# Gathering the value products of a retention pair, and zeros ahead of the first projection, in a two-layer hybrid encoder

## The chip, the core and the metric

The kernel runs on one core of one Trainium2 chip. The metric is the device time of one execution in microseconds (us), lower is better. Before the change it is 1287.65 us, the median of three runs (1287.47 to 1289.41).

## What is computed

Two encoder layers act on x with 512 positions and 1024 channels. Each layer first projects RMSNorm(x) with one matrix into retention queries, keys, values and gates (eight heads of 64 channels) and into queries, keys and values of four differential-attention heads. The retention is written in chunks; within a chunk every head needs masked scores times values, and a state from the other chunks is added:

```python
scores = jnp.einsum('bnthd,bnshd->bnhts', qc, kc) * dmask[None, None]
intra = jnp.einsum('bnhts,bnshd->bnthd', scores, vc)
...
out = (intra + cross_f + cross_b).reshape(B, S, H, D)
```

Both groups are normed per head, joined and projected back (`w_out`), then a SwiGLU block with 2816 inner channels follows. All is float32.

## The kernel before, in words

Activations lie transposed, channels on the partitions, so x is eight tiles of 128x512. For most products a float32 operand is split in two, hi (a rounded copy of type fp32r, made by ACT in `split_chunk` L166, `split_scaled` L185 or `split` L192) and lo (the rest, made by DVE in L167, L186, L193). `mm3` (L173 to L176) then issues three fp32r products for each, hi*hi, hi*lo and lo*hi. Weights come in chunks of 128x1024 through three `raw` buffers, all issued from SP's queue (L152).

A layer has five stages. `project_first` makes four projections from the eight tiles of x, interleaved, while these still arrive: for each tile 12 products of 512 columns, 96 in all. In layer 0 the loads for it are issued at L661 to L668, alternating half a weight chunk (L152) and a tile of x (L115), after the load of the parameters `prm_sb` (L109); all are on SP. The rows of the norm follow (L223), then attention heads woven with the other projections (L586). Then comes the **retention stage**: L617 weaves the generator `pairs` with fillers, which are the remaining projections (`acc` banks) and the first half of the output projection (L604, also `acc` banks). The second half of the output projection (L623) needs the results `mix[0]` to `mix[3]` of the four pairs, and the feed-forward block (L629 on) needs the output projection.

`ret_pair` (L404) handles two heads and yields after each of its steps. Step 1 (to L436) makes the decay weights, the state `r` from a float32 product (L430), and the split queries and keys. Step 2 (L439 to L460) makes for each head a mask `arg` (L442 to L444), and then, for each half c of the 512 positions, eight score products (L454) into two `sc` banks, one a head, and two maskings on DVE (L457), one a head, into a tile `sm`. Tiles `sm` come from the ring `ah` of three buffers. Step 3 (L462 to L476) opens the bank `o` with two float32 products of the state (L463, L464) and adds the eight value products (L469): for each half c and each chunk j one for head 0, which writes partitions 0 to 63 of the bank, and one for head 1, which writes partitions 64 to 127. They are plain float32, 64 columns of weights, 256 columns moved. The trace records each float32 product as two matmuls, so a pair's eight value products are 16 records, and the two layers' eight pairs have 128. Step 4 (L478 on) squares, sums over partitions (L128, L129), norms, gates (L481, L482) and splits the result into `mix`.

`PAIRS` (L36) interleaves these steps over the pairs. What order an engine's queue has in the end is not set by the order of the code alone: the program is built by a planner with a simulated clock (L756), which issues on each engine, in order of the code, what is ready at that moment of the simulation. A dependency made with `order` (L94) asks for an order in the plan alone; it puts no wait on the chip. The data dependencies carry the waits.

PSUM has four tags of two banks: `acc`, `sc`, `o` and `aux`.

Of the kernel before, what the change touches and what calls it, by code (L numbers as in the profile page):

```python
# [9 lines left out]
F32R = mybir.dt.float32r  # L10
# [3 lines left out]
P = 128  # L14
# [22 lines left out]


NW, NQK, NMIX, NAH, NHL = 12, 11, 20, 3, 3


PRM_AG, PRM_FG, PRM_RG, PRM_QG, PRM_KG, PRM_DG = 0, 16, 32, 34, 36, 38
# [9 lines left out]
def encoder_kernel(ctx: ExitStack, tc: tile.TileContext, xT, wfirst, wsingle, wvv, wout, wgu, wdn, prm, lam, cst, outT):  # L52
    nc = tc.nc
# [10 lines left out]
    def nm(s):  # L64
        uid[0] += 1
        return f"{s}{uid[0]}"

    def big(s, dt=F32, tag="w", bufs=NW):
        return tpool.tile([P, T], dt, tag=tag, name=nm(s), bufs=bufs)
# [4 lines left out]
    def bank(tag, bufs):  # L74
        return psum.tile([P, 512], F32, tag=tag, name=nm(tag), bufs=bufs)
# [4 lines left out]
    aux_bank = lambda: bank("aux", 2)  # L80
# [8 lines left out]
    def f32(ap):  # L89
        return ap.bitcast(F32)  # L90
# [3 lines left out]
    order = mybir.DependencyInfo(mybir.DependencyClass.NoSync, mybir.DependencyReason.DATA)  # L94
# [11 lines left out]


    prm_sb = cpool.tile([P, PRM_N], F32, name="prm_sb")
    nc.sync.dma_start(prm_sb, prm)  # L109
    cst_sb = cpool.tile([P, CST_N], F32, name="cst_sb")  # L110
    xscr = ctx.enter_context(tc.tile_pool(name="dpool", bufs=1, space=bass.MemoryType.DRAM)).tile([KT, P, T], F32, name="xscr")

    def load_x(src, kt):
        xt = big("x", tag="qk", bufs=NQK)
        nc.sync.dma_start(xt, src[kt])  # L115
        return xt

    ndist = cst_sb[:, CST_DIST : CST_DIST + 896]
# [38 lines left out]
            load_piece(new, src, i)  # L157
        return new

    def split_chunk(raw, n, pieces):  # L160
        hi = wpool.tile([P, 1024], F32R, tag="hi", name=nm("hi"), bufs=NHL)
        lo = wpool.tile([P, 1024], F32R, tag="lo", name=nm("lo"), bufs=NHL)
        q = n // pieces
        for i in range(pieces):
            s = slice(i * q, (i + 1) * q)
            nc.scalar.copy(hi[:, s], raw[:, s])  # L166
            nc.vector.tensor_tensor(lo[:, s], raw[:, s], f32(hi[:, s]), op=ALU.subtract)  # L167
        return hi, lo

    def chunk(*a, **kw):  # L170
        return split_chunk(*load_chunk(*a, **kw))

    def mm3(out, L, R, start, stop):  # L173
        nc.tensor.matmul(out, L[0], R[0], start=start, stop=False)  # L174
        nc.tensor.matmul(out, L[0], R[1], start=False, stop=False)  # L175
        nc.tensor.matmul(out, L[1], R[0], start=False, stop=stop)  # L176

    def cut(pair, *idx):
        return tuple(t[idx] for t in pair)
# [99 lines left out]
    def layer(l, n1, h, x_src, first_raw):  # L279


        def project_first():
            banks = [b() for b in (acc_bank, acc_bank, sc_bank, sc_bank)]
            for c in range(4):
                w = [t.rearrange("p (k f) -> p k f", f=512) for t in split_chunk(*first_raw[c])]
                for k in range(2):
                    kt = 2 * c + k
                    for i, ps in enumerate(banks):
                        mm3(ps, cut(w, slice(None), k, slice(i * P, (i + 1) * P)), h[kt], kt == 0, kt == KT - 1)
            return banks  # L290
# [8 lines left out]
        first = project_first()  # L299
# [104 lines left out]
        def ret_pair(pr):  # L404
            qT, kT, v = rqs[pr], rks[pr], rv
            lgc = lambda d, hh: lg[:, l * 16 + d * 8 + 2 * pr + hh : l * 16 + d * 8 + 2 * pr + hh + 1]
            lgp = lambda d: lg[:, 32 + l * 8 + d * 4 + pr : 32 + l * 8 + d * 4 + pr + 1]

            wq = big("wq")
            func(wq[:, :C], qpos[:, :C], AF.Exp, scale=lgp(1))  # L410
            func(wq[:, C:], qpos[:, C:], AF.Exp, scale=lgp(0))
            qw = wq
            nc.vector.tensor_tensor(qw, qT, wq, op=ALU.mult)

            tp = aux_bank()
            for j in range(4):
                nc.tensor.transpose(tp[:, j * P : (j + 1) * P], kT[:, j * P : (j + 1) * P], ident)
            kw = big("kw")
            nc.vector.tensor_tensor(
                kw.rearrange("p (j h d) -> p j h d", j=4, h=2),  # L420
                tp.rearrange("p (j h d) -> p j h d", j=4, h=2),
                wk[:, l, :, 2 * pr : 2 * pr + 2].rearrange("p j (h o) -> p j h o", o=1).broadcast_to([P, 4, 2, HD]),
                op=ALU.mult,
            )
            kv = aux_bank()
            e = slice((pr % 2) * P, (pr % 2 + 1) * P)
            for d in range(2):
                for j in range(2):
                    jj = 2 * d + j
                    nc.tensor.matmul(kv[:, d * P : (d + 1) * P], kw[:, jj * P : (jj + 1) * P], v[pr // 2][jj][:, e], start=j == 0, stop=j == 1)  # L430
            r = rs[pr % 2]
            kvv = kv[:, : 2 * P].rearrange("p (d e) -> p d e", d=2)
            for hh in range(2):
                b = slice(hh * HD, (hh + 1) * HD)
                nc.vector.tensor_copy(r[b, :, b], kvv[b, :, b])
            qs, ks = stack_one(qT, "mix", NMIX), stack_two(kT, "mix", NMIX)  # L436
            yield

            both = []  # L439
            for hh in range(2):  # L440
                arg = big("arg")
                nc.vector.tensor_scalar(arg[:, :384], dneg, lgc(1, hh), None, op0=ALU.mult)  # L442
                nc.vector.scalar_tensor_tensor(arg[:, :384], dpos, lgc(0, hh), arg[:, :384], op0=ALU.mult, op1=ALU.add)
                func(arg[:, :384], arg[:, :384], AF.Exp)  # L444
                both.append(bass.AP(arg.tensor, arg.offset, [arg.ap[0], [P, 2], [1, C]]))
            s = []
            for c in range(2):
                ps = [sc_bank() for _ in range(2)]
                for j in range(2):
                    for hh in range(2):  # L450
                        out = ps[hh][:, (1 - j) * C : (2 - j) * C]
                        sb, tb = slice((2 * c + j) * P, (2 * c + j + 1) * P), slice(c * C, (c + 1) * C)
                        for part in range(2):
                            nc.tensor.matmul(out, ks[hh][part][:, sb], qs[hh][:, tb], start=part == 0, stop=part == 1)  # L454
                sm = tpool.tile([P, 2, T], F32, tag="ah", name=nm("sm"), bufs=NAH)
                for hh in range(2):
                    nc.vector.tensor_tensor(  # L457
                        sm[:, hh].rearrange("p (j t) -> p j t", j=2), ps[hh].rearrange("p (j t) -> p j t", j=2), both[hh], op=ALU.mult
                    )
                s.append(sm)  # L460
            yield
            o = out_bank()  # L462
            nc.tensor.matmul(o[:, :C], r[:, 1, :], qw[:, :C], start=True, stop=False, skip_group_check=True)  # L463
            nc.tensor.matmul(o[:, C:], r[:, 0, :], qw[:, C:], start=False, stop=False, skip_group_check=True)  # L464
            for c in range(2):
                for j in range(2):
                    for hh in range(2):
                        b = slice(hh * HD, (hh + 1) * HD)
                        nc.tensor.matmul(  # L469
                            o[b, c * C : (c + 1) * C],  # L470
                            v[pr // 2][2 * c + j][:, (pr % 2) * P + hh * HD : (pr % 2) * P + (hh + 1) * HD],
                            s[c][:, hh, (1 - j) * C : (2 - j) * C],
                            start=False,
                            stop=(c == 1 and j == 1),
                            skip_group_check=True,
                        )  # L476
            yield
            ss = aux_bank()  # L478
            sq = square_sums(ss, consts["bones_r"], o)
            rsqrt(sq, ss, 1.0 / HD)  # L480
            nc.vector.scalar_tensor_tensor(sq, o, prm_sb[:, PRM_RG + l : PRM_RG + l + 1], sq, op0=ALU.mult, op1=ALU.mult)  # L481
            nc.vector.tensor_tensor(sq, sq, gates[pr], op=ALU.mult)  # L482
            mix[pr] = split(sq, "mix", NMIX)
            yield "norm"
# [60 lines left out]
        q, k = [None] * 4, [None] * 4  # L545
# [83 lines left out]
        for a0, a1 in FFN:  # L629
            act = []  # L630
            for ff in range(a0, a1):
                pgu = []
                for gu in range(2):
                    w = [t.rearrange("p (k f) -> p k f", f=P) for t in chunk(wgu[l, ff, gu])]
# [12 lines left out]
            for m in range(KT):  # L647
                w = chunk(wdn[l, m][:, a0 * P : a1 * P], (a1 - a0) * P)
# [12 lines left out]
    n, h, raws = Norm(), [], []  # L661
    for kt in range(KT):
        if kt % 2 == 0:
            raws.append(new_chunk(1024, 2))
        load_piece(raws[-1], wfirst[0, kt // 2], kt % 2)
        xt = load_x(xT, kt)
        h.append(split_scaled(xt, prm_sb[:, PRM_AG + kt : PRM_AG + kt + 1], "h", 16))
        n.add(xt)  # L668
    for l in range(DEPTH):
        if l:  # L670
            raws = [load_chunk(wfirst[l, c]) for c in range(4)]
        n, h = layer(l, n, h, xT if l == 0 else xscr, raws)
# [87 lines left out]
```

## Time and profile before

| | us |
|---|---|
| median of 3 runs | 1287.65 |
| the profiled execution | 1287.41 |
| its span, first to last instruction | 1285.6 |
| PE busy in it | 1271.1 |
| DVE busy | 769.2 |
| ACT busy | 570.5 |

The span is the time between the first and the last instruction; the execution's own time has 1.8 us around it. PE is the matmul engine, PEld its weight load, DVE the vector engine, ACT the scalar engine, POOL the general engine, SP the queue that issues transfers. Matmuls are pipelined: a record of 0.39 us can be followed by the next 0.23 us later, so prices below are taken from start to start.

### The profile page before, as it was taken

To read this page: it belongs to the slowest core of one execution; us is meant where nothing else is said; L and a number is where in the kernel's file an instruction comes from. 1 tells how busy PE (TensorE), PEld (TensorE's weight loads), DVE (VectorE), ACT (ScalarE), POOL (GpSimd) and SP (SyncE) were. 2 spreads that over 40 slices of the span, in tenths; PEclk is the share of its full clock that TensorE was granted. 3 is DMA by queue.
4 is the path that set the end of the run, shared out by engine and by line. 5 is a ranking of instruction groups with operands and counts; after the bars stand their busy time and mean duration, and the time that the engine had idled before them with its cause. 6 is when DMAs were issued, how large, how long until landed. Compare 5 with 4: busy or idle time off the path is not lost.

```text
span 1285.6 us, 15670 instructions
## 1 busy us (share of the span) xinstructions
PE 1271.1 (99%) x6192; PEld 1055.3 (82%) x6192; DVE 769.2 (60%) x1191; ACT 570.5 (44%) x887; POOL 17.3 (1%) x38
## 2 busy tenths in 40 slices
PE   8999999999999999999999999999999999999998
PEld 6888998678888888888888889977788888888887
DVE  6899759857443444344648997687664434443443
ACT  6777646544321222123438785564543223221221
POOL 1000000000000000000000000000000000000000
PEclk9999999999999999999999999999999999999999
DMA  7222224112333332332432122141233333333322
GB/s 263 82 67 66 67 66 148 36 64 98 99 94 103 99 98 82 114 91 85 160 109 83 50 83 66 56 141 50 66 101 96 98 98 98 98 98 98 93 80 90
DMA packets 36793, 120.07 MB, mean 93 GB/s; under 512 B 4208, under 2 KB 4208, under 8 KB 36592
## 3 DMA queue, kind: packets, MB, share of 16 engines
q1 hardware_dynamic: 36720, 119.08, 29.5%
q8 instruction: 48, 0.79, 0.3%
q14 instruction: 25, 0.20, 0.0%
HBM read 114.87 MB, written 4.19 MB: 93 GB/s over the span
## 4 chain that ended last, share of the span: by engine, by line
PE 97%; DVE 1%; ACT 1%; issue 0%; DMA 0%; SPq 0%
PE acc L174 15%; PE acc L175 14%; PE acc L176 14%; PE o L174 8%; PE o L176 8%; PE o L175 8%; PE sc L174 7%; PE sc L176 7%; PE sc L175 7%; PE sc L369 2%; PE o L469 2%; PE sc L454 1%; PE aux L385 1%; PE aux L128 1%; PE aux L129 1%; PE aux L430 1%
## 5 line engine op out<-in xcount | busy, mean ns | idle before, releaser
L166 ACT CAST hi<-raw 128x1024 fp32r<-128x1024 f32 (+2 forms) x212 | 215.7, 1019 | 510.0 <-issue 154.9
L174 PE MATMUL acc<-hi,hi 128*128 128x512 f32 (+1 forms) x914 | 337.3, 370 | 5.9 <-ACT hi L185 5.6
L175 PE MATMUL acc<-lo,hi 128*128 128x512 f32 (+1 forms) x914 | 338.3, 370 | 0.0
L176 PE MATMUL acc<-hi,lo 128*128 128x512 f32 (+1 forms) x914 | 337.7, 370 | 0.0
L167 DVE TENSOR_TENSOR lo<-raw,hi 128x1024 fp32r<-128x1024 f32 (+2 forms) x212 | 250.3, 1182 | 45.3 <-ACT hi L166 44.9
L174 PEld LDWEIGHTS acc<-hi,hi 128*128 128x128 f32 x914 | 172.6, 189 | 36.3 <-ACT hi L185 5.6
L175 PEld LDWEIGHTS acc<-lo,hi 128*128 128x128 f32 x914 | 172.5, 189 | 29.6 <-issue 1.2
L176 PEld LDWEIGHTS acc<-hi,lo 128*128 128x128 f32 x914 | 172.6, 189 | 29.2 <-issue 1.2
L174 PE MATMUL o<-hi,hi 128*128 128x512 f32 (+1 forms) x438 | 163.8, 374 | 2.2 <-DVE sq L481 2.2
L175 PE MATMUL o<-lo,hi 128*128 128x512 f32 (+1 forms) x438 | 163.6, 374 | 0.0
L176 PE MATMUL o<-hi,lo 128*128 128x512 f32 (+1 forms) x438 | 163.6, 374 | 0.0
L174 PE MATMUL sc<-hi,hi 128*128 128x512 f32 x408 | 159.4, 392 | 0.3 <-ACT hi L166 0.3
L176 PE MATMUL sc<-hi,lo 128*128 128x512 f32 x408 | 159.3, 390 | 0.0
L175 PE MATMUL sc<-lo,hi 128*128 128x512 f32 x408 | 159.2, 390 | 0.0
L174 PEld LDWEIGHTS o<-hi,hi 128*128 128x128 f32 x438 | 82.3, 188 | 17.6 <-DVE sq L481 2.7
L175 PEld LDWEIGHTS o<-lo,hi 128*128 128x128 f32 x438 | 82.4, 188 | 14.7
L176 PEld LDWEIGHTS o<-hi,lo 128*128 128x128 f32 x438 | 82.3, 188 | 14.6
L174 PEld LDWEIGHTS sc<-hi,hi 128*128 128x128 f32 x408 | 76.9, 189 | 18.6 <-issue 1.5
L176 PEld LDWEIGHTS sc<-hi,lo 128*128 128x128 f32 x408 | 76.9, 188 | 16.1
L175 PEld LDWEIGHTS sc<-lo,hi 128*128 128x128 f32 x408 | 76.9, 188 | 15.9
L103 ACT ACTIVATE sc<-sc,mx 128x512 f32<-128x512 f32 x64 | 46.0, 720 | 16.8 <-DVE mx L373 16.4
L599 DVE TENSOR_TENSOR x<-x,acc 128x512 f32<-128x512 f32 x36 | 24.6, 685 | 39.4 <-PE acc L176 39.3
(133 smaller groups left out, 1289.1 us busy)
## 6 DMA issues: line engine op xcount, KB each, us to landing
raw<-in_wgu SPq DMA_DIRECT2D x88, 512.0 KB, 3.5
raw<-in_wsingle SPq DMA_DIRECT2D x32, 512.0 KB, 3.5
raw<-in_wdn SPq DMA_DIRECT2D x32, 512.0 KB, 3.5
raw<-in_wvv SPq DMA_DIRECT2D x16, 512.0 KB, 3.5
raw<-in_wout SPq DMA_DIRECT2D x16, 512.0 KB, 3.6
raw<-in_wdn SPq DMA_DIRECT2D x16, 384.0 KB, 3.2
x<-in_xT SPq DMA_DIRECT2D x16, 256.0 KB, 4.2
raw<-in_wfirst SPq DMA_DIRECT2D x8, 256.0 KB, 5.2
```

Source lines behind the costliest of these rows:

```text
L103: i = nc.scalar.activation(out, src, f, **kw).ins
L128: nc.tensor.matmul(ps, w, hi, start=True, stop=False)
L129: nc.tensor.matmul(ps, w, lo, start=False, stop=True)
L166: nc.scalar.copy(hi[:, s], raw[:, s])
L167: nc.vector.tensor_tensor(lo[:, s], raw[:, s], f32(hi[:, s]), op=ALU.subtract)
L174: nc.tensor.matmul(out, L[0], R[0], start=start, stop=False)
L175: nc.tensor.matmul(out, L[0], R[1], start=False, stop=False)
L176: nc.tensor.matmul(out, L[1], R[0], start=False, stop=stop)
L369: nc.tensor.matmul(ps, q[m][:, t], k[m][part], start=part == 0, stop=part == 1)
L385: nc.tensor.transpose(tp[:, j * P : (j + 1) * P], a[:, j * P : (j + 1) * P], ident)
L469: nc.tensor.matmul(o[b, c * C : (c + 1) * C], v[pr // 2][2 * c + j][:, (pr % 2) * P + hh * HD : (pr % 2) * P + (hh + 1) * HD], s[c][:, hh, ...
L599: nc.vector.tensor_tensor(xt, xt, ps, op=ALU.add)
```

## The change

- In `ret_pair` the names of the four maskings of a pair (two halves, two heads) are kept, and each of the eight value products gets an `order` dependency on all four.
- A tile `warm` of 128x512 zeros is written by DVE, and nine fp32r products of it (512 columns each, into an `aux` bank) are put first in the code of PE.
- The parameters' load and the load of the first tile of x are issued from ACT's queue instead of SP's.
- The hi copy of the first half weight chunk of layer 0 is made by DVE (`tensor_copy`) instead of ACT.

```diff
--- before.py
+++ after.py
@@ -38,6 +38,8 @@
 
 NW, NQK, NMIX, NAH, NHL = 12, 11, 20, 3, 3
 
+NWARM = 9
+
 
 PRM_AG, PRM_FG, PRM_RG, PRM_QG, PRM_KG, PRM_DG = 0, 16, 32, 34, 36, 38
 PRM_DEC, PRM_DECP = 40, 72
@@ -106,13 +108,19 @@
 
 
     prm_sb = cpool.tile([P, PRM_N], F32, name="prm_sb")
-    nc.sync.dma_start(prm_sb, prm)
+    nc.scalar.dma_start(prm_sb, prm)
+
+    warm = big("warm", F32R)
+    nc.vector.memset(f32(warm), 0.0)
+    warm_bank = aux_bank()
+    for i in range(NWARM):
+        nc.tensor.matmul(warm_bank, warm[:, :P], warm, start=True, stop=True)
     cst_sb = cpool.tile([P, CST_N], F32, name="cst_sb")
     xscr = ctx.enter_context(tc.tile_pool(name="dpool", bufs=1, space=bass.MemoryType.DRAM)).tile([KT, P, T], F32, name="xscr")
 
-    def load_x(src, kt):
+    def load_x(src, kt, queue=None):
         xt = big("x", tag="qk", bufs=NQK)
-        nc.sync.dma_start(xt, src[kt])
+        (queue or nc.sync).dma_start(xt, src[kt])
         return xt
 
     ndist = cst_sb[:, CST_DIST : CST_DIST + 896]
@@ -157,13 +165,16 @@
             load_piece(new, src, i)
         return new
 
-    def split_chunk(raw, n, pieces):
+    def split_chunk(raw, n, pieces, first=False):
         hi = wpool.tile([P, 1024], F32R, tag="hi", name=nm("hi"), bufs=NHL)
         lo = wpool.tile([P, 1024], F32R, tag="lo", name=nm("lo"), bufs=NHL)
         q = n // pieces
         for i in range(pieces):
             s = slice(i * q, (i + 1) * q)
-            nc.scalar.copy(hi[:, s], raw[:, s])
+            if first and i == 0:
+                nc.vector.tensor_copy(hi[:, s], raw[:, s])
+            else:
+                nc.scalar.copy(hi[:, s], raw[:, s])
             nc.vector.tensor_tensor(lo[:, s], raw[:, s], f32(hi[:, s]), op=ALU.subtract)
         return hi, lo
 
@@ -282,7 +293,7 @@
         def project_first():
             banks = [b() for b in (acc_bank, acc_bank, sc_bank, sc_bank)]
             for c in range(4):
-                w = [t.rearrange("p (k f) -> p k f", f=512) for t in split_chunk(*first_raw[c])]
+                w = [t.rearrange("p (k f) -> p k f", f=512) for t in split_chunk(*first_raw[c], first=l == 0 and c == 0)]
                 for k in range(2):
                     kt = 2 * c + k
                     for i, ps in enumerate(banks):
@@ -443,7 +454,7 @@
                 nc.vector.scalar_tensor_tensor(arg[:, :384], dpos, lgc(0, hh), arg[:, :384], op0=ALU.mult, op1=ALU.add)
                 func(arg[:, :384], arg[:, :384], AF.Exp)
                 both.append(bass.AP(arg.tensor, arg.offset, [arg.ap[0], [P, 2], [1, C]]))
-            s = []
+            s, masked = [], []
             for c in range(2):
                 ps = [sc_bank() for _ in range(2)]
                 for j in range(2):
@@ -454,9 +465,10 @@
                             nc.tensor.matmul(out, ks[hh][part][:, sb], qs[hh][:, tb], start=part == 0, stop=part == 1)
                 sm = tpool.tile([P, 2, T], F32, tag="ah", name=nm("sm"), bufs=NAH)
                 for hh in range(2):
-                    nc.vector.tensor_tensor(
+                    i = nc.vector.tensor_tensor(
                         sm[:, hh].rearrange("p (j t) -> p j t", j=2), ps[hh].rearrange("p (j t) -> p j t", j=2), both[hh], op=ALU.mult
                     )
+                    masked.append(i.ins.name)
                 s.append(sm)
             yield
             o = out_bank()
@@ -466,7 +478,7 @@
                 for j in range(2):
                     for hh in range(2):
                         b = slice(hh * HD, (hh + 1) * HD)
-                        nc.tensor.matmul(
+                        i = nc.tensor.matmul(
                             o[b, c * C : (c + 1) * C],
                             v[pr // 2][2 * c + j][:, (pr % 2) * P + hh * HD : (pr % 2) * P + (hh + 1) * HD],
                             s[c][:, hh, (1 - j) * C : (2 - j) * C],
@@ -474,6 +486,9 @@
                             stop=(c == 1 and j == 1),
                             skip_group_check=True,
                         )
+
+                        for name in masked:
+                            tc.add_manual_dep(i.ins, name, order, reason="values of a pair together")
             yield
             ss = aux_bank()
             sq = square_sums(ss, consts["bones_r"], o)
@@ -663,7 +678,7 @@
         if kt % 2 == 0:
             raws.append(new_chunk(1024, 2))
         load_piece(raws[-1], wfirst[0, kt // 2], kt % 2)
-        xt = load_x(xT, kt)
+        xt = load_x(xT, kt, nc.scalar if kt == 0 else None)
         h.append(split_scaled(xt, prm_sb[:, PRM_AG + kt : PRM_AG + kt + 1], "h", 16))
         n.add(xt)
     for l in range(DEPTH):
```

## Rows read from the trace of the kernel before

**Rows 1.** The page: busy time of the engines, and the chain that ended last.

```profile
PE 1271.1 (99%) x6192; PEld 1055.3 (82%) x6192; DVE 769.2 (60%) x1191; ACT 570.5 (44%) x887; POOL 17.3 (1%) x38
...
PE 97%; DVE 1%; ACT 1%; issue 0%; DMA 0%; SPq 0%
```

**Rows 2.** Windows: stretch, length, PE, PEld, DVE, ACT, POOL busy, clock, DMA share, GB/s.

```profile
210.00:227.00 17.00, 17.00 (x96) 12.88 (x95) 15.18 (x25) 8.07 (x14) 1.56 (x3) 1.00 0.36 111
227.00:240.00 13.00, 13.00 (x66) 8.93 (x64) 11.63 (x19) 7.37 (x13) 0.52 (x1) 1.00 0.12 40
240.00:252.00 12.00, 12.00 (x62) 8.45 (x61) 9.61 (x17) 5.85 (x10) 0.52 (x1) 1.00 0.16 46
252.00:264.00 12.00, 12.00 (x59) 8.01 (x58) 6.04 (x9) 2.69 (x4) 0.00 (x0) 1.00 0.15 44
```

**Rows 3.** Line 469 alone: its records, and PE's idle time just before them.

```profile
L469 PE MATMUL o<-sm,rv x128: 379/379/430, 216.4 to 900.1; 128*64 128x256 f32 x128
...
  DVE sm L457: 0.4, 1
```

**Rows 4.** Timeline of PE, layer 0: start, time; a row of two records, one of six.

```profile
228.96 0.28 PE L454 MATMUL sc<-q,khi 128*128 128x256 f32 x1
229.08 0.28 PE L454 MATMUL sc<-q,klo 128*128 128x256 f32 x1
229.29 0.65 PE L469 MATMUL o<-sm,rv 128*64 128x256 f32 x2
229.86 0.50 PE L176 MATMUL acc<-hi,lo 128*128 128x512 f32 x1
230.20 0.39 PE L174 MATMUL acc<-hi,hi 128*128 128x512 f32 x1
230.43 0.40 PE L175 MATMUL acc<-lo,hi 128*128 128x512 f32 x1
...
239.15 1.08 PE L469 MATMUL o<-sm,rv 128*64 128x256 f32 x6
240.16 0.39 PE L454 MATMUL sc<-q,khi 128*128 128x256 f32 x1
```

**Rows 5.** Timeline of PE, layer 1: rows of eight and of four records.

```profile
866.78 1.08 PE L469 MATMUL o<-sm,rv 128*64 128x256 f32 x8
867.80 0.66 PE L417 MATMUL aux<-cst_sb,rk 128*128 128x128 f32 x4
...
894.57 0.65 PE L469 MATMUL o<-sm,rv 128*64 128x256 f32 x4
895.15 0.50 PE L175 MATMUL acc<-lo,hi 128*128 128x512 f32 x1
```

**Rows 6.** Timeline of PE, layer 1: the end of the retention stage.

```profile
909.51 0.50 PE L174 MATMUL o<-hi,hi 128*128 128x512 f32 x1 [2.23 <-DVE sq L481]
```

**Rows 7.** Timeline, the first 31 us: loads, the first splits, the first projection.

```profile
1.65 0.42 SPq L115 DMA_DIRECT2D x<-in_xT  x1
...
4.60 0.69 DVE L167 TENSOR_TENSOR lo<-raw,hi 128x512 fp32r<-128x512 f32 x1 [1.23 <-ACT hi L166]
4.81 0.72 ACT L185 ACTIVATE hi<-x,prm_sb 128x512 fp32r<-128x512 f32 x1 [0.24 <-DMA x<-in_xT]
...
5.59 1.22 PE L174 MATMUL acc<-hi,hi 128*128 128x512 f32 x2 [5.59 <-ACT hi L185]
...
9.16 0.63 PE L175 MATMUL sc<-lo,hi 128*128 128x512 f32 x1
...
9.59 0.63 PE L176 MATMUL sc<-hi,lo 128*128 128x512 f32 x1
...
30.22 0.39 PE L128 MATMUL aux<-hi,ones_r 128*128 128x512 f32 x1
```

**Rows 8.** Window of the first products, columns as in rows 2.

```profile
5.50:11.50 6.00, 5.91 (x14) 4.71 (x15) 5.14 (x8) 5.62 (x11) 0.00 (x0) 1.00 1.02 372
```

**Rows 9.** Lines of DVE, 227 to 276 us: maskings; busy, mean ns, idle before.

```profile
L457 DVE TENSOR_TENSOR sm<-sc,arg 128x512 f32<-128x512 f32 x11 | 7.6, 688 | 5.7 <-PE sc L454 5.7
```

## The prediction, made before the change was run

> **What bounds the kernel.** I read the page first. PE is busy for 99% of the span and holds 97% of the chain that ended last; DVE is busy for 60%, ACT for 44% [rows 1]. So a microsecond that PE no longer needs is a microsecond of the end, as long as PE then finds other work. Next I read windows of layer 0's retention stage. PE is full in each, but DVE stands at 15.18 of 17 us, 11.63 of 13 and 9.61 of 12, and falls to half only after 252 us [rows 2]. This is the place to watch: if PE gets faster here, DVE is next. Then I read the timeline of PE around line 469, the value products, for what is lost there although PE counts as busy. Last come the start, where PE stands idle, and the ends of the two retention stages.
>
> **The value products.** A pair's eight products are 16 records, and all eight pairs have 128 [rows 3]. In the timeline they stand in 32 uninterrupted rows: 16 of two records, 12 of six, two of eight and two of four. I take prices from start to start. A row of two (one product) lasts 0.57 us, 229.29 to 229.86; one of six 1.01 us [rows 4]. A row of eight lasts 1.02 us and one of four 0.58 us [rows 5]. So four records cost what two do, and eight what six do: the products of the two heads write different halves of the bank and run together when they are neighbours. A row costs 0.58 us for its first pair of products and 0.44 us for each further pair, (1.02 - 0.58). A lone product takes a whole place.
>
> A row also costs something at its ends. From the last score product to the row are 0.21 us (229.08 to 229.29), while that product's like before took 0.12; and the product behind the row keeps the next one for 0.34 us (229.86 to 230.20), where 0.23 is normal [rows 4]. That is 0.09 and 0.11, 0.2 us a row.
>
> Before: 16 x 0.58 + 12 x 1.01 + 2 x 1.02 + 2 x 0.58 = 24.6 us, and 32 x 0.2 = 6.4 us at the ends, 31.0 in all. After, if each pair's 16 records stand in one row: 0.58 + 3 x 0.44 + 0.2 = 2.1 us, eight times, 16.8 us. **The rows give 14.2 us.**
>
> Not all rows will stay whole. The dependency asks only that the planner issues the products after the four maskings; it does not forbid other work in between. Before, three or four products came free together 16 times, and the planner left 14 of these groups whole and cut the other two in three places. Those groups have 35 inner gaps (12 x 2 + 2 x 3 + 2 + 3), so about one gap in twelve is cut. Eight rows with seven gaps each would have some five cuts. A cut costs the ends and a dearer first pair, 0.2 + 0.14 = 0.34 us, and up to 0.44 more where it parts a pair. I take 5 x 0.34 = 1.7 us off, with bounds of 0 and 5 x 0.78 = 3.9. That leaves 12.5 us.
>
> **What waits longer.** A value product of the first half used to need one masking, and now stands behind four. The row is queued in order on PE, so whatever the planner puts behind it waits with it. The bank `o` is opened no earlier than before, but step 4 of the pair starts after a row of 1.9 us where 1.0 us followed the last masking: 0.9 us later. The tiles `sm` of both halves are held until the row, so of three buffers one is left for the next pair's first half, and its second half cannot be masked before the row. DVE gets no work here. Fillers cover all of this while they last. At the end of the stage they run out: in layer 1 PE then stood idle for 2.2 us, waiting for the last pair's norm [rows 6], in layer 0 hardly at all. With 6 to 7 us less of PE work in each stage, the last pair's chain must shorten as much or PE idles for the rest. I take 1 us more idle time in each layer (the 0.9 us from above), 2 us, with bounds of -2 (the idle time of layer 1 goes away) and the whole gain of the rows. What is late next at this place is the last `mix` tile, for the second half of the output projection.
>
> **The start.** PE's first product starts at 5.59 us, when ACT has split the first tile of x, whose load was issued third, at 1.65 us, and arrived at 4.81 [rows 7]. Products of 512 columns then follow each other every 0.43 us (9.16 to 9.59) [rows 7], which is 1.2 GHz; later every 0.23 us, near 2.4 GHz [rows 4]. The granted clock is given as 1.00 even in the stretch of the 14 slow products [rows 8], so the spacing has to tell it here. The sum agrees: 5.59 + 14 x 0.43 + 82 x 0.227 = 30.2, where the next stage's first product starts, at 30.22 [rows 7].
>
> The nine products of zeros need a memset of 512 columns on DVE, whose queue is otherwise nearly empty then. No row shows such a memset; a pass of DVE over 512 columns takes 0.69 us [rows 7], and nothing is the other bound. I take 0.5, so that they start at about 1.5 us. Nine at 0.43 us end at 5.4. The first load of x is now second on ACT's queue instead of third on SP's, one issue of 0.42 us earlier [rows 7], and ACT goes to it at once, without the first cast, so the real products could start at about 5.1; they start at 5.4. SP's own queue moves up by two issues, 0.8 us, and so do all loads in it. The DVE copy (some 0.6 to 0.69 us by the same row) and the `lo` behind it end near 4.9 us, before the first `lo` product is due. The two issues on ACT stand ahead of its first split, but ACT waits for that tile's transfer anyway; without this cover they would cost 0.8 us. If PE's faster clock comes as much earlier as its work does, 4.1 us (at 7.5 instead of 11.6), five real products run at 0.43 and 91 at 0.227: 5.4 + 2.1 + 20.7 = 28.2 us. **The start gives 2.0 us**; bounds are 3.3 (5.1 and no slow product) and -0.3 (the zeros end at 5.9, the clock rises no earlier). The tiles of x need no more time than PE takes: a tile is 12 products, 2.7 us, while ACT and DVE need under 2 us for each.
>
> The Trainium skill ("TensorE: Matmul & The Clock Gate", Part 1) speaks against a fixed gain: the number of slow matmuls at the start differs between runs of one kernel, 6, 11 or 14 in its example. No run here shows that; the three times lie 1.9 us apart. By it, with six slow products instead of 14 before, the kernel would have been 8 x 0.2 = 1.6 us faster, and the start would give 0.4 us.
>
> **Sum.** 1287.41 (the profiled execution, 0.24 under the median) - 14.2 + 1.7 + 2.0 - 2.0 = 1274.9; against the median 1275.1. I say 1275.
>
> **Rivals.** *DVE takes over.* From 210 to 252 us it is busy 36.4 of 42 us [rows 2]. Of the rows, 11 of layer 0's 17 lie there, some 11/17 of 7 us, so PE would want 37.5 us. DVE would have to run at 97% with a chain of short steps. For it speaks that, and the single free `sm` buffer; against it, that DVE waits for the score products, 5.7 us before 11 maskings [rows 9], a wait that shrinks with PE, and that DVE is half idle after 252 us. If half of the rows' gain turns into idle time at the stages' ends: 1275 + 6 = 1281.
>
> *Rows that wait.* If the planner's clock has the maskings earlier than the chip does, PE stands before each row with everything behind it. Twelve and a half us over eight rows, with the start's 2.0 less 2.0 for the tails, are 1.6 us a row, over two maskings of 0.69 us [rows 9]: from there on the change loses. Standing still for all four, 2.75 us, gives eight times 2.75 less 12.5, that is 1287.4 + 9.5 = 1297. Against it: before, PE waited for a masking at one record of 128, 0.4 us [rows 3], though it also stood just behind the maskings. The Trainium skill (the same page, Part 3, "The mechanism") states that matmuls start and end strictly in order, which is the rule by which such a wait would hold everything; the timelines here show no product overtaking.
>
> *Nothing gathers.* If the planner does not hold the products back, or cuts the rows as before, only the start's 2.0 us remain: 1285.6.
>
> **How the numbers follow.** Rows and start as summed: 0.62, from 1270.5 (no cuts, no more idle time) to 1278. DVE or the tails take half: 0.22, 1278 to 1283.5. Nothing gathers: 0.07. Rows that wait: 0.08. The rest, 0.01, is faster still. A measurement of this kernel can tell about 0.2%, 2.6 us, from no change, so "nothing gathers" counts as the same. Faster 0.85, same 0.07, slower 0.08. The range is 1270.5 to 1282.5, the first case and most of the second.
>
> **What would show it.** Right: some eight to 13 rows on line 469, most of 16 records and 1.9 us; the first products of the second stage near 28.2 us; idle time of PE at the stages' ends of 2 to 5 us together. Wrong: idle time of PE before line 469 put down to the maskings; more than 20 rows; PE idle over 3 us at the end of either stage; DVE at over 95% before 252 us.

## The result, and the profile after

The changed kernel takes 1274.38 us (median of four runs, 1273.27 to 1275.50), the kernel before in the same series 1287.56 (1286.57 to 1289.41). The ratio is 0.9896, with a 95% interval of 0.9879 to 0.9913: faster by 1.0%. The forecast was 1275. The profiled execution took 1275.36 us, 12.05 less than that of before.

The page after, to be read against [rows 1]:

```profile
PE 1264.8 (99%) x6201; PEld 1056.9 (83%) x6201; DVE 769.7 (60%) x1193; ACT 569.8 (45%) x886; POOL 17.3 (1%) x38
...
PE 97%; DVE 1%; ACT 1%; DMA 0%; issue 0%; SPq 0%
```

PE has nine more matmuls, the zeros, and is still the bound. The shares tell nothing of the change; one has to go to the lines. The value products are now line 481. Timeline of PE, layer 0, to be read against [rows 4, 5]:

```profile
220.21 1.08 PE L481 MATMUL o<-sm,rv 128*64 128x256 f32 x8
221.23 0.50 PE L186 MATMUL acc<-lo,hi 128*128 128x512 f32 x1
221.66 0.65 PE L481 MATMUL o<-sm,rv 128*64 128x256 f32 x2
222.24 0.39 PE L465 MATMUL sc<-q,khi 128*128 128x256 f32 x1
...
222.79 1.08 PE L481 MATMUL o<-sm,rv 128*64 128x256 f32 x6
223.79 0.39 PE L465 MATMUL sc<-q,khi 128*128 128x256 f32 x1
...
248.38 1.51 PE L481 MATMUL o<-sm,rv 128*64 128x256 f32 x10
249.82 0.50 PE L186 MATMUL acc<-lo,hi 128*128 128x512 f32 x1
...
258.59 1.95 PE L481 MATMUL o<-sm,rv 128*64 128x256 f32 x16
```

A pair's 16 records stand in one row only three times in the two layers. The other five pairs are cut, three into 8, 2 and 6 records, two into 10 and 6. That makes 16 rows instead of 32: three of 8 records, three of 2, five of 6, two of 10 and three of 16. From start to start they take 3 x 1.02 + 3 x 0.58 + 5 x 1.01 + 2 x 1.44 + 3 x 1.88 = 18.4 us, and with 0.2 us at the ends of each 21.6. Before it was 31.0. **The rows gave 9.4 us.**

Waits of PE in the changed kernel, 195 to 300 us and 840 to 920 us (engine and line, what it waited for, us in total, times, longest):

```profile
PE acc L185 <- ACT hi L177: 0.3, 1, 0.3
...
PE sc L185 <- ACT hi L177: 0.3, 1, 0.3
```

The 2.23 us of idle time at the end of layer 1's stage [rows 6] are gone; what is left are two waits of 0.3 us for a weight chunk, which the kernel before has too. **That gave 2.2 us.** Timeline of PE there, first before, to be read with [rows 6], then after: the last row of value products, the second product of the last pair's sums, and the first product behind the norm.

```profile
899.37 1.08 PE L469 MATMUL o<-sm,rv 128*64 128x256 f32 x6
...
906.89 0.40 PE L129 MATMUL aux<-lo,bones_r 128*128 128x512 f32 x1
```

```profile
888.63 1.95 PE L481 MATMUL o<-sm,rv 128*64 128x256 f32 x16
...
894.74 0.40 PE L137 MATMUL aux<-lo,bones_r 128*128 128x512 f32 x1
...
897.37 0.50 PE L185 MATMUL o<-hi,hi 128*128 128x512 f32 x1
```

From the sums to that product it is 2.6 us in both. It writes the bank `o` that DVE's step of the norm has just read (`sq`, L481 before, 908.71 to 909.46 us); ACT makes the pair's `mix` tile only after that, from 910.22 us, so what PE waited for is the bank and not the result. Before, the plan had no other product left for this time; now it puts the sums 4.2 us behind the row instead of 6.5, and other products fill it.

DVE, in windows to be read against [rows 2] (columns as there), came closer to its limit, 16.17 of 17 us from 210 to 227 and 11.20 of 12 us from 240 to 252, and PE stayed full:

```profile
210.00:227.00 17.00, 17.00 (x99) 13.35 (x98) 16.17 (x28) 9.30 (x16) 1.55 (x3) 1.00 0.39 115
...
240.00:252.00 12.00, 12.00 (x65) 8.90 (x65) 11.20 (x19) 6.20 (x10) 0.52 (x1) 1.00 0.14 46
252.00:264.00 12.00, 12.00 (x65) 9.32 (x65) 6.49 (x10) 4.10 (x7) 0.00 (x0) 1.00 0.13 44
```

The start, to be read against [rows 7] (timeline of ACT and PE):

```profile
1.66 1.28 ACT L101 ACT_TABLE_LOAD   x1 [1.66 <-PEq L767]
4.17 0.24 ACT L105 ACTIVATE lg<-prm_sb 128x48 f32<-128x48 f32 x1 [1.22 <-DMA prm_sb<-in_prm]
5.07 0.62 ACT L177 CAST hi<-raw 128x512 fp32r<-128x512 f32 x1 [0.66 <-DMA raw<-in_wfirst]
5.59 0.72 ACT L196 ACTIVATE hi<-x,prm_sb 128x512 fp32r<-128x512 f32 x1
...
1.46 4.21 PE L117 MATMUL aux<-warm 128*128 128x512 f32 x9 [1.46 <-DVE eps_sb L151]
...
6.36 1.22 PE L185 MATMUL acc<-hi,hi 128*128 128x512 f32 x2 [0.70 <-ACT hi L196]
...
9.09 0.63 PE L186 MATMUL acc<-lo,hi 128*128 128x512 f32 x1
9.51 0.63 PE L187 MATMUL acc<-hi,lo 128*128 128x512 f32 x1
...
30.19 0.39 PE L136 MATMUL aux<-hi,ones_r 128*128 128x512 f32 x1
```

The zeros ran from 1.46 us on, as forecast. But the first real product started at 6.36 us, 0.8 later than before. The first tile of x landed 4.1 us after its issue at 1.17 us, so near 5.3 us and 0.5 later than before; and ACT's split of it, at 5.59, stood behind a cast that waited for its weights until 5.07 us. The products still ran at 0.43 us each until 10.4 us. The second stage begins at 30.19 us, where it was 30.22. **In this execution the start gave nothing.** Together 9.4 and 2.2 make 11.6 of the 12.05 us; the rest was not traced.

### The profile page after: what moved, and what is told of

It is laid out like the page before. It is cut to its first block, busy times and chain, and to the rows that moved or that the text cites. A ratio compares the mean times of both kernels' runs of the same rounds, so it can differ in the third digit from the quotient of the medians.

```text
span 1273.5 us, 15689 instructions
## 1 busy us (share of the span) xinstructions
PE 1264.8 (99%) x6201; PEld 1056.9 (83%) x6201; DVE 769.7 (60%) x1193; ACT 569.8 (45%) x886; POOL 17.3 (1%) x38
## 4 chain that ended last, share of the span: by engine, by line
PE 97%; DVE 1%; ACT 1%; DMA 0%; issue 0%; SPq 0%
PE acc L185 15%; PE acc L186 15%; PE acc L187 15%; PE o L185 8%; PE o L187 8%; PE o L186 8%; PE sc L185 7%; PE sc L187 7%; PE sc L186 7%; PE sc L380 2%; PE o L481 1%; PE sc L465 1%; PE aux L396 1%; PE aux L137 1%; PE aux L136 1%; PE aux L441 1%
## 5 line engine op out<-in xcount | busy, mean ns | idle before, releaser
L105 ACT ACTIVATE sc<-sc,mx 128x512 f32<-128x512 f32 x64 | 46.0, 720 | 16.8 <-DVE mx L384 16.4
```

The lines of the kernel that those rows point to most:

```text
L105: i = nc.scalar.activation(out, src, f, **kw).ins
```

## The experiments

All are edits of the changed kernel. The second stage's first product (line 136, before 128) marks what the start gave; 30.22 us is the mark of before [rows 7]. Each ratio is to runs of the kernel before on the same chip (medians 1287.31, 1287.45 and 1287.20 in the three series).

| kernel | median, range (us) | ratio [95%] | second stage | rows |
|---|---|---|---|---|
| gathered only | 1275.23, 1275.06 to 1275.61 | 0.9902 [0.9887, 0.9917] | 29.94 | 16 |
| start only | 1287.08, 1285.47 to 1287.64 | 0.9992 [0.9983, 1.0001] | 28.08 | 32 |
| gathered, zeros, loads as before | 1273.06, 1272.92 to 1273.29 | 0.9885 [0.9871, 0.9898] | 27.79 | 16 |
| chained | 1275.38, 1274.41 to 1276.49 | 0.9903 [0.9889, 0.9916] | 30.23 | 8 |
| chained, sums first, loads as before | 1266.93, 1266.91 to 1267.41 | 0.9841 [0.9827, 0.9856] | 27.76 | 8 |
| 12 zeros | 1273.70, 1273.16 to 1273.99 | 0.9892 [0.9875, 0.9908] | 28.90 | 16 |
| no zeros | 1275.26, 1274.99 to 1275.67 | 0.9906 [0.9891, 0.9920] | 30.59 | 16 |
| 12 zeros, loads as before | 1273.68, 1273.29 to 1273.90 | 0.9893 [0.9878, 0.9907] | 28.17 | 16 |
| zeros only | 1286.70, 1284.72 to 1287.28 | 0.9994 [0.9985, 1.0002] | 27.54 | 32 |
| the changed kernel again | 1274.38, 1273.20 to 1275.62 | 0.9899 [0.9884, 0.9914] | 30.51 | 16 |

**Gathering alone.** The zeros go, and loads and cast are put back as they were:

```diff
-    for i in range(NWARM):
-        nc.tensor.matmul(warm_bank, warm[:, :P], warm, start=True, stop=True)
...
-    nc.scalar.dma_start(prm_sb, prm)
+    nc.sync.dma_start(prm_sb, prm)
...
-        xt = load_x(xT, kt, nc.scalar if kt == 0 else None)
+        xt = load_x(xT, kt)
```

> Only the order dependency of the value products; no zeros, loads and casts as before. Theory 1 (all of the gain of the profiled execution comes from the retention stages: in the changed kernel the products stand in 16 rows that cost 18.3 us and 16 x 0.2 at their ends, 21.5 where 31.0 stood, and PE's idle time at the stages' ends falls by some 2.6): 16 rows, first product at 5.59 us, the second stage at 30.2 us, about 12 us less than before, 1275.4. Rival (the zeros and the reordered loads carry 2 us of the gain on average): 1277 to 1278, and the second stage 2 us later than in the changed kernel. Rival 2 (the vanished idle time comes from the shifted start): 2.6 us more, 1278, with 2 us idle at the end of layer 1's stage.

1275.23 us, 12.1 below before. The rows are cut at the same places, and neither stage ends in an idle time over 0.5 us. So both the rows' gain and the vanished idle time belong to the order dependency, and rival 2 falls. Of the rival's 2 us from the start, the medians leave 0.9 us (1274.38 against 1275.23, in different series).

**The start alone.** The order dependency goes, the rest stays:

```diff
-                        for name in masked:
-                            tc.add_manual_dep(i.ins, name, order, reason="values of a pair together")
```

> The zeros, the two loads on ACT's queue and the cast on DVE, without the order dependency. Theory 1 (the start gives nothing, because the first real product is 0.8 us later than before, which eats what the earlier clock gives): 32 rows as before, 0 to 1 us less than before, 1286.6 to 1287.6, first real product at 6.4 us. Rival (the start gives the 2 us of the forecast in most executions): 1285.5.

The median is 0.2 us under before, and the interval holds no change. But the executions reach from 1285.5 to 1287.6, and in the profiled one, the best of them (1285.47), the second stage began at 28.08 us, near the forecast's 28.2 but by another way: the first real product was late there too (6.19 us), and none was slow. So the mechanism exists. That it does not come in every execution is shown by the profile of the changed kernel (30.19 us). In this kernel it is read from the times alone: the slower executions show a mean granted clock of 0.999 to 1.000, as the faster ones do, which speaks against a fall of the clock later on.

**Zeros with the loads as before.**

```diff
-    nc.scalar.dma_start(prm_sb, prm)
+    nc.sync.dma_start(prm_sb, prm)
...
-        xt = load_x(xT, kt, nc.scalar if kt == 0 else None)
+        xt = load_x(xT, kt)
```

with the first cast on ACT again.

> The order dependency and the zeros, but both loads on SP's queue and the first cast on ACT, as before. Theory (the moved loads made the first real product late: the load of the first tile landed at 5.3 instead of 4.8 us and its split stood behind a cast on ACT): the first real product is back at 5.6 us, the idle time behind the zeros is 0.3 us or less, PE's faster products begin by 10.5 us or sooner, and the second stage starts at 28.8 us or sooner, 1.4 us or more under the changed kernel: 1272 to 1273.5. Rival (the clock alone sets it, and it rises when it rises): second stage at 29.8 or later, at most 0.4 us under the changed kernel.

All four executions are within 0.4 us of each other, 2.2 us below gathering alone in the same series. Timeline of ACT and PE:

```profile
4.21 0.62 ACT L177 CAST hi<-raw 128x512 fp32r<-128x512 f32 x1 [1.31 <-DMA raw<-in_wfirst]
5.13 0.72 ACT L196 ACTIVATE hi<-x,prm_sb 128x512 fp32r<-128x512 f32 x1 [0.30 <-DMA x<-in_xT]
...
1.46 3.67 PE L117 MATMUL aux<-warm 128*128 128x512 f32 x9 [1.46 <-DVE warm L114]
5.90 0.73 PE L185 MATMUL acc<-hi,hi 128*128 128x512 f32 x2 [0.77 <-ACT hi L196]
...
6.93 0.39 PE L186 MATMUL acc<-lo,hi 128*128 128x512 f32 x1
7.17 0.39 PE L187 MATMUL acc<-hi,lo 128*128 128x512 f32 x1
...
27.79 0.39 PE L136 MATMUL aux<-hi,ones_r 128*128 128x512 f32 x1
```

The products follow each other every 0.23 us from the beginning, although PE stood idle for 0.77 us between the zeros and them. But the nine zeros took 3.67 us here and 4.21 in the changed kernel: in this execution the clock had risen before the last of them, ahead of the idle time. The two moved loads and the cast thus brought nothing: the first real product starts at 5.90 us here and 5.88 in the kernel that only gathers, but at 6.19 and 6.31 us in the two kernels of this series with moved loads. The landing times show why: the parameters needed 3.4 us from issue to landing on ACT's queue in the changed kernel and 1.7 on SP's before, the first tile of x 4.1 and 3.1; and ACT, in order, met the cast of the second half chunk before the tile of x. A likely reason for the later landing is that SP's loads moved up and are now under way at the same time; no run here shows that apart.

**Whole rows.** A pair's products are chained, the one that needs the last masking first:

```diff
+            last = None
-            for c in range(2):
+            for c in (1, 0):
...
-                    for hh in range(2):
+                    for hh in (1, 0):
...
+                        if last:
+                            tc.add_manual_dep(i.ins, last, order, reason="one row")
+                        last = i.ins.name
```

(`stop` moves to the product that is now the last.)

> The changed kernel, with a pair's eight value products chained in order, the one that needs the last masking first. Theory (the rows of the changed kernel are cut because the planner asks only that the maskings are issued, so that products of the second half still come free one by one): eight rows of 16 records, each 1.88 us, 15.0 and 8 x 0.2 us, 16.6 where the changed kernel has 21.5: 4.9 us less, 1269.5. Rival (a row that starts only behind the last masking makes the pair's norm late and PE idle at the stages' ends, 0.9 us or more in each layer): 3 us less at most, 1271.5, with 1 to 2 us idle before the second half of the output projection. Rival 2 (DVE takes over before 252 us): no gain, 1274.

Eight rows, as the first theory says, and yet no gain. Timeline and windows of PE at the end of layer 0's stage (columns of the last row as in rows 2):

```profile
255.66 1.95 PE L482 MATMUL o<-sm,rv 128*64 128x256 f32 x16
257.54 0.50 PE L185 MATMUL sc<-hi,hi 128*128 128x512 f32 x1
...
264.02 0.40 PE L137 MATMUL aux<-lo,bones_r 128*128 128x512 f32 x1
...
266.64 0.80 PE L185 MATMUL o<-hi,hi 128*128 128x512 f32 x1 [2.22 <-DVE sq L500]
...
266.00:270.00 4.00, 3.36 (x8) 2.71 (x9) 1.97 (x3) 0.62 (x1) 0.00 (x0) 0.58 0.02 4
```

The row ends at 257.5 us. The plan then gives PE 6.2 us of other products before the last pair's sums (263.79 and 264.02), and has nothing left to cover the norm behind them: 2.2 us idle, in layer 1 the same. In layer 0 the clock then fell: granted 0.58 of full on average from 266 to 270 us, and eight products at 0.43 instead of 0.23 us. The sum for the profiled executions: rows 21.6 - 8 x 2.08 = 5.0 less, idle time 4.4 more, the clock 8 x 0.2 = 1.6 more, together 1.0 more; measured 1276.49 - 1275.36 = 1.1. The rival on the tails is right, only larger than it said. The four executions lie in two pairs 2 us apart, 1274.4 to 1274.6 and 1276.2 to 1276.5 us, which the start's two levels (below) would give; all four show a mean granted clock of 0.998, which suggests that the fall is not in the profiled one alone.

**Whole rows and the sums first.** To this, with the loads as before, comes an order dependency for the output projection's second half, from its third tile on:

```diff
+            after = last_sum[0]
...
-                        mm3(ps, cut(w, slice(None), kt, slice((m % 2) * P, (m % 2 + 1) * P)), parts[kt], kt == 0, kt == 3)
+                        i = mm3(ps, cut(w, slice(None), kt, slice((m % 2) * P, (m % 2 + 1) * P)), parts[kt], kt == 0, kt == 3)
+                        if half == 1 and m > 1 and kt == 0:
+                            tc.add_manual_dep(i.ins, after, order, reason="sums of the last pair first")
```

(`last_sum` holds the name of the last partition sum's second product; `mm3` returns its first.)

> Chained products (eight rows of 16 records), loads and cast as before, nine zeros, and an order dependency that puts the partition sums of the last pair ahead of the second half of the output projection from its third tile on. Theory (the chain took 4.7 us from the rows and lost it again to 2.2 us of idle time at each stage's end, where the plan had spent the products that could have covered the last norm before its sums were issued, and to slow products behind one of these gaps): no idle time over 0.5 us at line 185 behind either stage, 4 to 5 us less than the gathered kernel with zeros and loads as before (1273.06): 1268 to 1269. Rival (the norm chain itself is too long for what is left to do): 1 to 2 us idle in each layer, 1270 to 1272.

Timeline of PE, the same place:

```profile
250.20 1.95 PE L484 MATMUL o<-sm,rv 128*64 128x256 f32 x16
252.07 0.51 PE L187 MATMUL sc<-lo,hi 128*128 128x512 f32 x1
...
254.04 0.39 PE L137 MATMUL aux<-hi,bones_r 128*128 128x512 f32 x1
...
254.74 0.39 PE L138 MATMUL aux<-lo,bones_r 128*128 128x512 f32 x1
254.97 0.39 PE L186 MATMUL acc<-hi,hi 128*128 128x512 f32 x1
```

The sums come 2.0 us behind the row, and the rest of the projection covers the norm: PE waits for nothing in this stage, and once for 0.3 us in the other layer's. 1266.93 us, 20.5 below before and 6.1 below the gathered kernel with the same start, whose cut rows account for 5.0 of it and its second wait of 0.3 us for 0.3; the remaining 0.8 was not traced. This version beats both kernels.

**The zeros.** Three kernels that differ in the zeros and the moved loads, the first with

```diff
-NWARM = 9
+NWARM = 12
```

> The changed kernel with 12 products of zeros instead of nine. Theory (the idle time of 0.7 to 0.9 us between the zeros and the first real product lets the faster clock come early in some executions and late in others, 2 us apart): without the gap all runs lie together at the level of the better ones, 1273.3, and the clock rises before 6.5 us; the first real product starts at about 6.7. Rival (the moment is chance, whatever the zeros do): two levels 2 us apart again. Rival 2 (zeros do not count, only real work): the clock rises at 10.5 us or later, 1275.5.

> The changed kernel without the zeros; loads on ACT's queue and the cast on DVE stay. Theory (the moved loads delay the first real product by 0.3 to 0.7 us, and without zeros the products start slow): first real product at 6.2 to 6.4 us, the second stage 0.3 us or more later than in the kernel that only gathers (1275.23), 1275.5 to 1276. Rival (the moved loads help): under 1275.2.

> Gathered products, 12 zeros, loads and first cast as before. Theory (three more zeros than needed delay the first real product): it starts at 6.6 instead of 5.9 us; the clock has risen by then, so 0.7 us more than with nine zeros (1273.06), 1273.5 to 1273.8, all runs on one level. Rival (the gap still costs the clock there too): 1272.5.

With 12 zeros and moved loads the four executions lie within 0.8 us, and the first real product starts without idle time at 6.75 us; all lie within 0.8 us of the better level of the changed kernel, and none at the other. The clock rose only with the first real products, though, later than expected. Without zeros but with moved loads the first real product comes at 7.03 us, later than expected; yet the kernel that only gathers has the same median (1275.26 and 1275.23), so neither the theory nor the rival got its time. Between the two profiled executions the second stage begins 0.65 us later and the time is 0.6 us longer, as the theory has it. With 12 zeros and loads as before 0.6 us are lost against nine, because the first real product waits for the zeros until 6.39 us.

**Zeros alone, and the changed kernel again.** The first has neither order dependency nor moved loads.

> The kernel before with nine products of zeros put in front, and nothing else. Theory (with loads and cast as before the zeros bring the faster clock forward in every execution): first real product at 5.6 to 5.9 us, second stage at 27.8 us, 2.2 to 2.4 us less than before, 1285.1, all runs within 1 us, 32 rows. Rival (the two levels of the changed kernel come with the zeros themselves): two levels 2 us apart, median 1286 or more.

> The changed kernel once more, beside the other. Theory (moved loads with nine zeros leave the moment of the faster clock open): two levels again, near 1273.4 and 1275.4, while the kernel with zeros alone keeps to one. Rival (the two levels of the first four runs came from the chip): one level.

The changed kernel shows two levels again: in both series together four executions at 1273.2 to 1273.4 us and four at 1275.4 to 1275.6. Both of its profiled ones are of the upper level and have slow products still at 9.9 us. But zeros alone do not keep to one level either; that expectation failed, with 1284.7 to 1287.3 us. Its profiled execution (1286.21), in which the first real product followed the zeros without idle time, shows one cause: the start is as good as forecast, 27.54 us, and most of the gain is lost again at the end of layer 1's stage. Timeline of PE and a window (columns as in rows 2):

```profile
904.21 0.40 PE L137 MATMUL aux<-lo,bones_r 128*128 128x512 f32 x1
906.83 0.79 PE L185 MATMUL o<-hi,hi 128*128 128x512 f32 x1 [2.23 <-DVE sq L493]
907.42 0.63 PE L186 MATMUL o<-lo,hi 128*128 128x512 f32 x1
907.85 0.63 PE L187 MATMUL o<-hi,lo 128*128 128x512 f32 x1
...
906.00:911.00 5.00, 4.17 (x12) 3.32 (x13) 2.13 (x3) 0.62 (x1) 0.00 (x0) 0.66 0.00 0
```

This is the idle time of [rows 6], and here the clock falls behind it, to 0.66 of full on average in this window. In the profiled executions of the kernel before and of the start alone it does not. The mean granted clock of the other executions fits it: the six with 0.998 took 1286.7 to 1287.3 us, and the three at 1284.7 to 1285.0 have 0.999 or 1.000. The kernel before, too, shows 0.998 in three of the 15 executions of the first series (1287.8 to 1288.0 us). The kernels with gathered but unchained products have no such idle time, and with loads as before they spread by 0.4 to 0.6 us only.

## Why the prediction was right, step by step

The time was right, 1275 against 1274.38, and so was the cause: PE bounds the kernel, and what short rows cost there is the gain. That the time came out within 1 us is luck, though: three terms of the sum were off, and their errors cancel. Against the forecast the rows gave 3.1 us less, the ends of the stages 4.2 more and the start 2.0 less. None of the three signs named for being right came: there were 16 rows and not eight to 13, the second stage began at 30.19 us and not near 28.2, and the idle time left in the stages was 0.6 us and not 2 to 5.

- **The price of a row** was right. A whole row takes 1.88 us (255.66 to 257.54 in the chained kernel) where 1.90 was summed, and the chained kernel's account closes to 0.1 us. The Trainium skill ("TensorEngine Tiling (Array Packing)", Key Properties) says that a change of tiling mode drains the engine; the 0.2 us at the ends of each row agree with it, though no run here separates the drain from the step between float32 and fp32r.
- **The cuts** were undersized: 4.8 us (21.6 - 16.8) where 1.7 was taken, beyond the bound of 3.9. The step that failed is that the planner would issue the products once four maskings were done, and would cut rows only for other work. What the rows fit is that it holds them until the maskings are issued in its plan. The products of the first half are then free at once, and those of the second come free head by head, as before: 8, 2, 6. It is no wait on the chip. In the changed kernel the second half's maskings ran from 218.12 to 219.40 us, and the first row began at 220.21. All eight cuts of the five parted pairs lie at these two of a pair's seven gaps, behind the first half and behind the second half's first product, and the chain, which changes order alone, removes them. The plan itself was not read.
- **The ends of the stages** had the wrong sign: 2.0 us more idle time were taken, 2.2 us less measured. What I left out is that an order dependency makes a new plan, in which the last pair's sums stand elsewhere, in layer 1 at 4.2 us behind the row instead of 6.5. That the worry was sound is shown by the chained kernel, with 6.5 us again and 2.2 us idle in each layer. What decides is where the plan puts the sums.
- **The start** was put at 2.0 us and gave none in the two profiled executions of the changed kernel, and some 2 us in four of its other six, by their times. No execution of this better level was profiled. The step that failed is that ACT would go to the first tile of x at once and PE would start at 5.4 us, and that the faster clock would come earlier by the work put in front: it came at 10.4 us. The loads were costed at one issue less; their landing, and the order in which ACT takes a cast and a split, were not. The zeros did what was forecast where the loads stay on SP: 27.5 to 27.8 us against a forecast of 28.2.
- **The rivals.** DVE did not take over: 38.58 of the 42 us from 210 to 252 in the changed kernel, 92%, with PE full, and PE was still full at 40.09 us, 95%, in the fastest version. The sign set at 95%, then, would have been a false one. No row of the changed kernel stood waiting for its maskings.
- **Two slips** changed nothing. 12 of layer 0's 17 rows lie between 210 and 252 us, not 11, which puts DVE at 98% there in the rival's sum. And the terms named for the lower end of the range (no cuts, no more idle time) add up to 1271.2 us, not 1270.5.

The note cited from the Trainium skill ("TensorE: Matmul & The Clock Gate", Part 1), that the number of slow matmuls differs between runs, agrees with the two levels of the changed kernel. What sets the level there stays open, but the profiles point at the idle time behind the zeros. Six of them have nine zeros that were all slow. Where the idle time behind these was 0.64, 0.70 and 1.13 us (chained, the changed kernel twice), the products stayed slow until 10.4 to 10.8 us; where it was nothing, 0.17 and 0.52 us (zeros alone, sums first, start alone), they were fast from the beginning. In the seventh, gathered with zeros and the loads as before, 0.77 us did no harm, but there the clock had risen within the zeros. Six profiles that differ in other things too do not prove it.

## What to carry to other kernels

An order dependency on another engine's work can mean "issued in the plan" and not "done": to keep products in one row, chain them with the one that waits longest in front, and read the resulting order before trusting it. When PE is the bound, work saved shows up only if something covers the chain behind it, so look at what stands between the last row and the next wait, and move the short link that starts this chain ahead of the long filler. Moving a first load to another queue need not make it land earlier: here it was issued 0.5 us earlier and landed 0.5 us later. Look at landing times, not at issue times.

## What the runs showed that was not expected

An idle time of 2.2 us in the middle of the program is enough, in some executions, for the granted clock to fall: to 1.2 GHz for eight products in two profiles (chained, layer 0; zeros alone, layer 1), at a price of 1.6 us beside the idle time, while the same gap left the clock alone in the profiles of the kernel before, of the start alone and in layer 1 of the chained kernel. Products of zeros can raise the clock: with nine of them and the loads as before, real products ran at 0.23 us from their first pairs on in all three profiles, where without zeros they were slow until 10.2 us or later.
